# Two batches of triangular inverses on GpSimd, their closing transposes held back, and the latent attention's transfers on SyncE

## The chip, the cores and the metric

One core of a Trainium2 chip runs the whole program. The metric is device time in microseconds (us) for one execution, inputs to output.

The engines are TensorE (PE, with its weight loads as PEld), VectorE (DVE), ScalarE (ACT), GpSimd (POOL) and SyncE (SP). Each takes its instructions in its own program order; a scheduler that runs when the kernel is built fixes that order.

## The reference

Two networks run in series: a two-layer one (`first_block`), and then a diffusion-style one (`second_block`) whose even layer mixes a Gated DeltaNet, run in both directions over the sequence, with a latent attention (MLA). The change touches only that even layer. The part of it that matters, shortened:

```python
def delta_rule_chunked(q, k, v, g, beta, s0):
    ...
    m = jnp.where(strict, jnp.einsum('bhncd,bhnsd->bhncs', kb, kc) * decay, 0.0)
    tmat = lax.linalg.triangular_solve(m + eye, eye, lower=True, unit_diagonal=True)
    u = jnp.einsum('bhncs,bhnsv->bhncv', tmat, vb)
    w = jnp.einsum('bhncs,bhnsk->bhnck', tmat, kb * jnp.exp(gc)[..., None])
    ...
    def step(s, inp):
        v_new = u_i - jnp.einsum('bhck,bhkv->bhcv', w_i, s)
        o_i = jnp.einsum('bhck,bhkv->bhcv', qd_i, s) + jnp.einsum('bhcs,bhsv->bhcv', qk_i, v_new)
        s = s * gl_i[..., None, None] + jnp.einsum('bhck,bhcv->bhkv', kd_i, v_new)

def even_mixer(...):
    o_lat, o_ctx = gdn_bidirectional(...)
    b_lat = blocked_attention(q_l, [k_c, k_l], [v_c, v_l], scale)
    b_ctx = blocked_attention(mla_q(ctx), k_c, v_c, scale)
    y = concatenate([gdn_output(o), b], -1) @ w_out
```

So for each chunk of 64 positions and each of 8 heads the inverse of a unit lower triangular 64x64 matrix is wanted; then a scan goes over the chunks and carries a state.

## The kernel before

Most of the kernel is dense matrix products on PE (`mm3`, L411 to L416). The even layer's stage lies at about 1500 to 1800 us of the span and comes in this order.

**Chunks.** The sequence is 4 blocks of 128 positions (numbers 0 to 3) and the context 2 more (4 and 5). `gdn_chunks` returns seven jobs, which run beside the last input projections (L416). `decays(b)` forms the triangles of block b for both directions and lays their diagonal 32x32 pieces out in a tile of `triW`, four blocks to a batch: batch "ctx" holds blocks 4 and 5 of both directions, batch 0 the blocks 0 to 3 forward, batch 1 the same backward. `triangles` (L1500) transposes a batch on DVE into a work tile A. `invert` (L1502 to L1515) turns A into its inverse X, for all 128 partitions at once: for each of 31 columns a multiply of two broadcast operands into `tm` (L1510) and a subtraction from X (L1511), 62 dependent instructions over tiles of 31 to 256 elements. Then it transposes X back into the batch's `triW` tile (L1513). All of that is on DVE.

A batch's tiles are lent by others. Batch 0 has A = `eo1` and X = `eo2`; batch 1 has A = a spare `triW` tile and X = `eo0`. `eo1` and `eo3` are also where the latent attention later writes its first result for the context.

**Scan.** `gdn_scan` makes four tiles `DT00`, `DT01`, `DT10`, `DT11` (direction, then parity of the walk), zeroed on GpSimd (L1527), and does six walks. Walk i takes one block in each direction. Its `solve` copies the inverted pieces into DT (L1546, ACT, 16 copies), transposes them (L1556, DVE), joins them by two groups of small products (`ng`, L1559 and L1563 on PE) with a copy `ND` (L1560, ACT) between and a copy with sign behind (L1565, ACT), and multiplies them into `sa` (L1575, PE), from which u and w follow. `kd` and `VK` are products on DVE (L1567, L1569). Then four `step`s, two in each direction, carry the states `St` (L1611 to L1633, PE and DVE in turn). Walks 0 and 1 take the context's blocks, so batch "ctx" alone; walk 2 is the first that needs batches 0 and 1.

**Filler.** `mla` is a generator of 12 units of the latent attention, and each walk draws one or two of them (`UNITS`), so that the attention's products lie beside the scan. A unit scores (`S`, L1402, PE), takes maxima and exponentials (L1328, L1332 on DVE; L1335 on ACT), transposes (`ptr`, L1348, PE; copied by ACT and DVE at L1351), weighs (`po`, L1359, PE), scales (`bt`, L1414 and L1415), and stores. Its operands `vp` and `kq` come by transfers that GpSimd issues (L1384, L1388), and its result goes out the same way (L1419) except in the context's units, where `hl` writes it as a high and a low part: a cast on ACT (L398) and a subtraction on DVE (L399), in the first into `eo1` and `eo3`.

The order around the change is the scheduler's. It is a program order for each engine, worked out with estimated durations, and an instruction that waits holds all that stand behind it on its engine.

Of the kernel before, what the change touches and what calls it, by code (L numbers as in the profile page):

```python
# [12 lines left out]
OP = mybir.AluOpType  # L13
# [225 lines left out]
def build(tc, A, out, cst_at, vec_at, chk_at, tap=None, upto=99, mark=lambda n: None):  # L239
    nc = tc.nc  # L240
    V, S, T, G = nc.vector, nc.scalar, nc.tensor, nc.gpsimd
# [11 lines left out]
    def load(dst, src):  # L253
        nc.sync.dma_start(dst, src)
# [358 lines left out]
    x = xp.tile([128, KD, SEQ], F32, name="x", tag="x")  # L613
# [464 lines left out]
    kqD = dram("kqD", [8, 96, 2, TOT])  # L1078
    vD = dram("vD", [4, 128, 6, 128])
    boD = dram("boD", [4, 128, TOT])  # L1080
# [299 lines left out]
    def mla(tp, ctx):  # L1380
        scale = 96.0 ** -0.5
        for p in range(4):
            vp = tp.tile([128, 6, 128], F32, name="vp", bufs=2)
            G.dma_start(vp, vD[p])  # L1384
            KQ = []
            for half in range(2):
                kq = tp.tile([96, 2, TOT], F32, name="kq", bufs=2)
                G.dma_start(kq, kqD[2 * p + half])  # L1388
                KQ.append(kq)
            for qb0, nk, k0, b0 in ((SEQ, CTX, SEQ, 4), (0, TOT, 0, 0), (256, TOT, 0, 0)):  # L1390
                Ps = []
                rsum = tp.tile([128, 4], F32, name="rsum", bufs=3)
                for half in range(2):
                    mx = tp.tile([128, 4], F32, name="mx", bufs=3)
                    row = [tp.tile([128, TOT], F32, name="P", bufs=8)[:, :nk] for _ in range(2)]

                    def score(i):
                        q = KQ[half][:, 1, qb0 + 128 * i:qb0 + 128 * i + 128]
                        for c0 in range(0, nk, 512):
                            c1 = min(c0 + 512, nk)  # L1400
                            pS = bank("S", c1 - c0, "S")
                            T.matmul(pS, q, KQ[half][:, 0, k0 + c0:k0 + c1], start=True, stop=True)  # L1402
                            yield pS

                    soft_rows(row, score, scale, mx, [rsum[:, c:c + 1] for c in (half, 2 + half)])
                    Ps.append(row)
                po = bank("out", 256, "po")
                for _ in weigh(po, Ps, [[(128 * j, 128)] * 2 for j in range(nk // 128)],
                               lambda half, j: vp[:, b0 + j, 64 * half:64 * half + 64], tp, "turn"):
                    pass  # L1410
                V.reciprocal(rsum, rsum)
                rb = on_features(rsum, 2, [256], "turn")[0]
                bt = tp.tile([128, 256], F32, name="bt", bufs=2)
                S.copy(bt, po)  # L1414
                V.tensor_tensor(bt, bt, rb, OP.mult)  # L1415
                if qb0 == SEQ:
                    hl(bt, *(v[:, p] for v in ctx))
                else:
                    G.dma_start(boD[p, :, qb0:qb0 + 256], bt)  # L1419
                yield  # L1420

    batches, batch, inverse, NOc = {}, {}, {}, []

    def off_diagonal(d, a):

# [4 lines left out]
    def gdn_chunks(gp, slots):  # L1430
# [70 lines left out]

        def invert(key, A, X, Y):  # L1502

            parts = batches[key][1]
            V.memset(X, 0.0)
            V.memset(X.rearrange("p y x -> p (y x)")[:, ::33], 1.0)
            for j in range(31):
                n, m = j + 1, 31 - j
                t = gp.tile([128, 256], F32, name="tm", bufs=1)[:, :n * m].rearrange("p (y x) -> p y x", y=m)
                V.tensor_tensor(t, X[:, j:j + 1, :n].to_broadcast([128, m, n]), A[:, n:, j:j + 1].to_broadcast([128, m, n]), OP.mult)  # L1510
                V.tensor_tensor(X[:, n:, :n], X[:, n:, :n], t, OP.subtract)  # L1511
            for d, r in parts:
                V.transpose(Y[r], X[r] if d == 0 else X[r].rearrange("p s c -> p c s"))  # L1513
            inverse[key] = Y

        def inversion(key, A, X):
            triangles(key, A)
# [5 lines left out]

    def gdn_scan(oT, gA, gp, beside, then):
        DTs = [[gp.tile([128, 8, 128], F32, name=f"DT{d}{i}") for i in range(2)] for d in range(2)]
        for t in DTs[0] + DTs[1]:
            G.memset(t, 0.0)  # L1527
        prep = {}

        def solve(i):  # L1530
# [69 lines left out]
        def step(d, b, a, St):  # L1600

            u, wT, kd, eb, qd, qk = prep[d, b]
            rows = halves[a]

            pb = bank("step", 1024, "st").rearrange("p (b c) -> p b c", b=2)
            pw, po, pu = pb[:, :, :256], pb[:, a, 256:], pb[:, 1 - a, 256:]
            for p in range(4):
                for r in halves:  # L1610
                    T.matmul(po[r, 64 * p:64 * p + 64], St[r, p], qd[r, p, rows], start=p == 0, stop=False)  # L1611
            for p in range(4):
                for half, r in enumerate(halves):
                    T.matmul(pw[rows, half, 64 * p:64 * p + 64], wT[r, p, rows], St[r, p], start=half != a, stop=half != a,
                             skip_group_check=half == a)
            vn = gp.tile([128, 8, 64], F32, name="vn", bufs=3)
            by = [v.rearrange("p (i b) t -> p i b t", b=2) for v in (vn[rows], u[rows])]
            V.tensor_tensor(by[0], by[1], pw[rows].rearrange("p b (i t) -> p i b t", i=4), OP.subtract)
            for h in range(8):
                T.matmul(pu[halves[h % 2], 64 * (h // 2):64 * (h // 2) + 64], kd[rows, h], vn[rows, h], start=True, stop=True)  # L1620
            for h in range(8):
                T.matmul(po[halves[h % 2], 64 * (h // 2):64 * (h // 2) + 64], vn[rows, h], qk[rows, 64 * h:64 * h + 64],
                         start=False, stop=h > 5)
            ot = oT[:, :, 128 * b + 64 * a:128 * b + 64 * a + 64]
            o3 = po.rearrange("p (i t) -> p i t", i=4)
            if (b, a) in seen:
                V.tensor_tensor(ot, o3, ot, OP.add)
            else:
                S.copy(ot, o3)
                seen.add((b, a))  # L1630
            last = 64 * a + (63 if d == 0 else 0)
            V.tensor_tensor(St, St, eb[:, :, last:last + 1].to_broadcast([128, 4, 64]), OP.mult)
            V.tensor_tensor(St, pu.rearrange("p (i t) -> p i t", i=4), St, OP.add)  # L1633

        St = []
        for d in range(2):
# [3 lines left out]
        order = [[4, 5, 0, 1, 2, 3], [5, 4, 3, 2, 1, 0]]  # L1640

        def walk(i):
            solve(i)
            for a in range(2):
                for d in range(2):
                    step(d, order[d][i], a if d == 0 else 1 - a, St[d])

        next(beside)
        for i in range(6):
            walk(i)  # L1650
# [525 lines left out]
```

## Time and profile before

| | us |
|---|---|
| median of 3 runs | 3222.15 |
| lowest, highest | 3220.92, 3222.18 |
| the profiled execution's own time | 3223.53 |
| its span | 3221.7 |
| busy PE, DVE, ACT, POOL | 3067.8, 2041.2, 1448.2, 17.4 |

The span is from the first to the last instruction of the profiled execution; 1.83 us of that execution's time lie outside it. Busy times are sums over instructions. Times in the rows below are us from the start of the span, and ns where marked as the mean of one.

### The profile page before, as it was taken

The page shows a single profiled execution, that of the slowest core. Times are in us where ns is not written, and L with a number is a line of the kernel's source. Part 1 is how long each engine was busy: PE and PEld are TensorE (multiplying, and loading weights), DVE is VectorE, ACT ScalarE, POOL GpSimd, SP SyncE. Part 2 cuts the span into 40 slices and gives each one's busy share as a digit, 9 for nine tenths or more (in the row PEclk, how much of TensorE's full clock was granted, in tenths as well). Part 3 has the DMA queues.
Part 4 walks back from the last instruction along what each step waited for, and adds up shares of the span by engine and source line. Part 5 has one row for each costly group of instructions (what it writes and reads, how often), then busy time and mean ns, then how long its engine had stood idle before and what let it go on. Part 6 is the DMA issues. An engine that isn't in the chain of part 4 may idle for free.

```text
span 3221.7 us, 51374 instructions
## 1 busy us (share of the span) xinstructions
PE 3067.8 (95%) x20678; PEld 2605.9 (81%) x20678; DVE 2041.2 (63%) x4021; ACT 1448.2 (45%) x2533; POOL 17.4 (1%) x47
## 2 busy tenths in 40 slices
PE   6999999998999999998899999999997989999998
PEld 5788888975888889876667898888887867898887
DVE  7976555788787777668966674442338347572335
ACT  4965333446553335556554562212124446562223
POOL 0000000000000000000100000000000000000000
PEclk9999999997999999998999999999998999999999
DMA  7556554320266554442322433441223221242232
GB/s 233 190 155 218 194 189 163 125 66 7 74 195 200 188 198 166 131 143 96 107 67 92 142 105 118 165 136 58 67 69 125 79 91 47 76 152 95 95 100 101
DMA packets 137615, 404.11 MB, mean 125 GB/s; under 512 B 13856, under 2 KB 37152, under 8 KB 136736
## 3 DMA queue, kind: packets, MB, share of 16 engines
q1 hardware_dynamic: 135344, 389.81, 36.6%
q0 software_dynamic: 2032, 11.01, 1.1%
q8 instruction: 162, 2.65, 0.3%
q14 instruction: 77, 0.63, 0.1%
HBM read 376.12 MB, written 24.64 MB: 124 GB/s over the span
## 4 chain that ended last, share of the span: by engine, by line
PE 62%; issue 8%; DVE 5%; ACT 4%; DMA 0%; POOL 0%; DVEq 0%; ACTq 0%; POOLq 0%
PE mm L416 49%; PE po L1359 2%; PE rb L547 2%; PE ptr L1348 1%; PE S L830 1%; PE S L1402 1%; PE ss L527 1%; ACT DT L1546 1%; ACT wH L398 1%; PE po L969 1%; PE sa L1575 1%; PE ptr L975 1%; DVE acc L519 1%; DVE wL L399 1%; DVE ct L1683 0%
## 5 line engine op out<-in xcount | busy, mean ns | idle before, releaser
L398 ACT CAST wH<-raw 128x1024 fp32r<-128x1024 f32 (+4 forms) x446 | 451.8, 1015 | 1144.7 <-PE mm L416 786.0
L399 DVE TENSOR_TENSOR wL<-raw,wH 128x1024 fp32r<-128x1024 f32 (+4 forms) x446 | 525.1, 1180 | 377.4 <-ACT wH L398 370.5
L416 PE MATMUL mm<-mH,wH 128*128 128x256 f32 (+1 forms) x1280 | 406.8, 340 | 8.2 <-DVE f L1764 5.8
L416 PE MATMUL mm<-mH,wL 128*128 128x256 f32 (+1 forms) x1280 | 404.1, 339 | 1.9 <-DVE wL L399 1.9
L416 PE MATMUL mm<-mL,wH 128*128 128x256 f32 (+1 forms) x1280 | 404.2, 338 | 0.0
L416 PEld LDWEIGHTS mm<-mH,wH 128*128 128x128 f32 x1280 | 230.7, 190 | 39.5 <-ACT wH L398 6.0
L589 DVE SCALAR_TENSOR_TENSOR raw<-raw,cond_c 128x1024 f32<-128x1024 f32 x128 | 156.6, 1225 | 157.1 <-DMA raw<-in_ada 156.4
L416 PEld LDWEIGHTS mm<-mH,wL 128*128 128x128 f32 x1280 | 229.7, 189 | 30.9 <-DVE wL L399 2.3
L416 PEld LDWEIGHTS mm<-mL,wH 128*128 128x128 f32 x1280 | 230.2, 189 | 28.6
L416 PE MATMUL mm<-f2u0L,wH 128*128 128x512 f32 (+1 forms) x752 | 190.3, 327 | 0.0
L416 PE MATMUL mm<-f2u0H,wH 128*128 128x512 f32 (+1 forms) x752 | 190.0, 326 | 0.0
L416 PE MATMUL mm<-f2u0H,wL 128*128 128x512 f32 (+1 forms) x752 | 189.6, 326 | 0.0
L416 PE MATMUL mm<-f2u1H,wL 128*128 128x512 f32 (+1 forms) x432 | 151.4, 352 | 1.2 <-DVE wL L399 1.1
L416 PE MATMUL mm<-f2u1H,wH 128*128 128x512 f32 (+1 forms) x432 | 150.9, 352 | 0.6 <-ACT nt L1739 0.5
L416 PE MATMUL mm<-f2u1L,wH 128*128 128x512 f32 (+1 forms) x432 | 151.2, 352 | 0.2
L416 PEld LDWEIGHTS mm<-f2u0H,wL 128*128 128x128 f32 x752 | 118.1, 189 | 13.1
L416 PEld LDWEIGHTS mm<-f2u0H,wH 128*128 128x128 f32 x752 | 117.6, 189 | 12.9
L416 PEld LDWEIGHTS mm<-f2u0L,wH 128*128 128x128 f32 x752 | 117.7, 189 | 12.6
L1744 DVE TENSOR_TENSOR nt<-nt,mm 128x512 f32<-128x512 f32 (+1 forms) x52 | 31.5, 605 | 146.8 <-PE mm L416 146.4
L626 DVE SCALAR_TENSOR_TENSOR x<-mm,mod,x 128x256 f32<-128x256 f32 (+1 forms) x112 | 66.1, 597 | 88.5 <-PE mm L416 88.3
L416 PE MATMUL mm<-f0L,wH 128*128 128x512 f32 (+1 forms) x296 | 107.0, 362 | 0.5 <-DVE f0L L565 0.5
L416 PE MATMUL mm<-f0H,wH 128*128 128x512 f32 (+1 forms) x296 | 106.8, 361 | 0.4 <-ACT f0H L564 0.4
(697 smaller groups left out, 7232.9 us busy)
## 6 DMA issues: line engine op xcount, KB each, us to landing
raw<-in_ada SPq DMA_DIRECT2D x192, 512.0 KB, 3.8
raw<-in_fw SPq DMA_DIRECT2D x142, 512.0 KB, 4.1
raw<-in_gw SPq DMA_DIRECT2D x113, 512.0 KB, 3.3
raw<-in_gw SPq DMA_DIRECT2D x34, 384.0 KB, 3.0
raw<-in_owin SPq DMA_DIRECT2D x25, 512.0 KB, 3.2
raw<-in_ewin SPq DMA_DIRECT2D x22, 512.0 KB, 3.3
raw<-in_awin SPq DMA_DIRECT2D x20, 512.0 KB, 3.9
raw<-in_ewout SPq DMA_DIRECT2D x18, 512.0 KB, 3.4
```

Source lines behind the costliest of these rows:

```text
L398: S.copy(H, src)
L399: V.tensor_tensor(L, src, H.bitcast(F32), OP.subtract)
L416: T.matmul(ps, W[w][:, k], h(p, k0 + k, sl), start=first and k == 0 and j == 0, stop=last and k == kt - 1 and j == 2)
L519: V.tensor_tensor(acc[0], acc[0], sq, OP.add)
L527: T.matmul(pc[:, ns * b:ns * b + ns], sq, sel, start=True, stop=True)
L547: T.matmul(pb[r * i:r * i + r, b:b + 128], rs[:, c:c + 1].to_broadcast([128, r]), ident, start=True, stop=True)
L589: V.scalar_tensor_tensor(junk, r, 1.0, c, OP.mult, OP.mult, accum_out=o[:, j:j + 1])
L626: V.scalar_tensor_tensor(x[:, n, sl], ps, gate[:, n:n + 1], x[:, n, sl], OP.mult, OP.add)
L830: T.matmul(ps, q, k[:, sl], start=j == 0, stop=j == 1)
L969: T.matmul(po[64 * half:64 * half + 64], vw[:, kt, :64], PT, start=kt == 0, stop=kt == b)
L975: T.transpose(pt[:, 128 * i:128 * i + 128], Ps[half][i][:, 128 * kt:128 * kt + 128], ident)
L1359: T.matmul(po[64 * half:64 * half + 64], vs[half], PT[:kn, half * w:half * w + w], start=j == 0, stop=j == len(keys) - 1)
```

## The change

1. `invert` works on GpSimd for batches 0 and 1; batch "ctx" stays on DVE. That covers the zeroing of X and the 62 instructions of each.
2. The closing transpose of batches 0 and 1 is put into a function and held in a list, `late`. Both are issued, on DVE, at the start of walk 2, and are ordered behind the last instruction of walk 1's last step.
3. Of the four DT tiles the two of even walks are zeroed on DVE, the two of odd walks on GpSimd as before.
4. `mla`'s loads of `vp` and `kq` and its stores of `bt`, 20 transfers, are issued by SyncE (`load`). In SyncE's order the first unit's `vp` and its two `kq` stand right behind the two loads of walk 1's k, and those wait for DVE's two `VK` products (L1567) of walk 0, whose buffers they take.

```diff
@@ mla @@
-            G.dma_start(vp, vD[p])
+            load(vp, vD[p])
...
-                G.dma_start(kq, kqD[2 * p + half])
+                load(kq, kqD[2 * p + half])
...
-                    G.dma_start(boD[p, :, qb0:qb0 + 256], bt)
+                    load(boD[p, :, qb0:qb0 + 256], bt)
...
-    batches, batch, inverse, NOc = {}, {}, {}, []
+    batches, batch, inverse, NOc, late = {}, {}, {}, [], []
@@ gdn_chunks, invert @@
-            parts = batches[key][1]
-            V.memset(X, 0.0)
-            V.memset(X.rearrange("p y x -> p (y x)")[:, ::33], 1.0)
+
+            E = V if key == "ctx" else G
+            E.memset(X, 0.0)
+            E.memset(X.rearrange("p y x -> p (y x)")[:, ::33], 1.0)
             for j in range(31):
                 n, m = j + 1, 31 - j
                 t = gp.tile([128, 256], F32, name="tm", bufs=1)[:, :n * m].rearrange("p (y x) -> p y x", y=m)
-                V.tensor_tensor(t, X[:, j:j + 1, :n].to_broadcast([128, m, n]), A[:, n:, j:j + 1].to_broadcast([128, m, n]), OP.mult)
-                V.tensor_tensor(X[:, n:, :n], X[:, n:, :n], t, OP.subtract)
-            for d, r in parts:
-                V.transpose(Y[r], X[r] if d == 0 else X[r].rearrange("p s c -> p c s"))
-            inverse[key] = Y
+                E.tensor_tensor(t, X[:, j:j + 1, :n].to_broadcast([128, m, n]), A[:, n:, j:j + 1].to_broadcast([128, m, n]), OP.mult)
+                E.tensor_tensor(X[:, n:, :n], X[:, n:, :n], t, OP.subtract)
+
+            def place():
+                for d, r in batches[key][1]:
+                    V.transpose(Y[r], X[r] if d == 0 else X[r].rearrange("p s c -> p c s"))
+                inverse[key] = Y
+            if key == "ctx":
+                place()
+            else:
+                late.append(place)
@@ gdn_scan @@
-        for t in DTs[0] + DTs[1]:
-            G.memset(t, 0.0)
+        for i in range(2):
+            for d in range(2):
+                (G if i else V).memset(DTs[d][i], 0.0)
...
+            return nc.cur_bb.bb.instructions[-1]
...
         def walk(i):
+            nonlocal done
+            if i == 2:
+                with tc.issue_after(done):
+                    for place in late:
+                        place()
             solve(i)
             for a in range(2):
                 for d in range(2):
-                    step(d, order[d][i], a if d == 0 else 1 - a, St[d])
+                    done = step(d, order[d][i], a if d == 0 else 1 - a, St[d])
```

The line numbers in the order rows below are those of each kernel: the changed kernel's L1511, L1512, L1516, L1535, L1554, L1564, L1568, L1573, L1586 are L1510, L1511, L1513, L1527, L1546, L1556, L1560, L1565, L1578 of the kernel before.

**GpSimd at the start of the scan.** Here are GpSimd's rows before; `vp` and `kq` are the attention's operands, and a number behind a name is a tile's.

```order
L1527 MEMSET DT00_14032 128x1024
L1527 MEMSET DT01_14033 128x1024
L1527 MEMSET DT10_14034 128x1024
L1527 MEMSET DT11_14035 128x1024
L1384 DMA vp_14044<-vD_t_10816 128x768
L1388 DMA kq_14046<-kqD_t_10813 96x1536
L1388 DMA kq_14048<-kqD_t_10813 96x1536
L1384 DMA vp_14975<-vD_t_10816 128x768
```

And here the same engine in the change, in the midst of batch 0's inverse (`eo2` is X, `eo1` is A):

```order
L1511 TENSOR_TENSOR tm_13849<-eo2_12714,eo1_12713 128x220
L1512 TENSOR_TENSOR eo2_12714<-eo2_12714,tm_13849 128x22x10
L1511 TENSOR_TENSOR tm_13852<-eo2_12714,eo1_12713 128x231
L1535 MEMSET DT01_14031 128x1024
L1512 TENSOR_TENSOR eo2_12714<-eo2_12714,tm_13852 128x21x11
L1535 MEMSET DT11_14033 128x1024
L1511 TENSOR_TENSOR tm_13855<-eo2_12714,eo1_12713 128x240
L1512 TENSOR_TENSOR eo2_12714<-eo2_12714,tm_13855 128x20x12
```

The zeroings of `DT01` and `DT11` now stand behind 21 and 22 of batch 0's 62 instructions, and no transfer stands in this queue any more.

**ScalarE at the context's first attention result.** Before, from the copy `bt` to the cast that writes `eo1` (walk 0's copies `eb`, `w_`, `wT` and `oT` stand between):

```order
L1414 COPY bt_14102<-po_14077 128x256
L1335 ACTIVATE P_14439,rsum_14437<-P_14439,mx_14438 128x768
L1591 ACTIVATE eb_14242<-eg_14233 128x512
L1335 ACTIVATE P_14440,rsum_14437<-P_14440,mx_14438 128x768
L1578 COPY w__14250<-sa_14251 128x256
L1578 COPY w__14250<-sa_14258 128x256
L1583 COPY wT_14270<-wt_14265 128x512
L1629 COPY oT_12710<-st_14285 128x4x64
L1335 ACTIVATE P_14458,rsum_14437<-P_14458,mx_14457 128x768
L1591 ACTIVATE eb_14281<-eg_14272 128x512
L1335 ACTIVATE P_14459,rsum_14437<-P_14459,mx_14457 128x768
L1629 COPY oT_12710<-st_14323 128x4x64
L1351 COPY PT_14482<-ptr_14477 128x512
L398 CAST eo1_14023<-bt_14102 128x256
```

In the change:

```order
L1335 ACTIVATE P_14437,rsum_14435<-P_14437,mx_14436 128x768
L1414 COPY bt_14100<-po_14075 128x256
L398 CAST eo1_14021<-bt_14100 128x256
L1599 ACTIVATE eb_14240<-eg_14231 128x512
L1335 ACTIVATE P_14438,rsum_14435<-P_14438,mx_14436 128x768
L1586 COPY w__14248<-sa_14249 128x256
L1586 COPY w__14248<-sa_14256 128x256
```

The cast stands right behind `bt`, 12 rows earlier, ahead of walk 0's `eb` and its second `w_`.

**VectorE and ScalarE at the entry to walk 2.** Before, DVE's closing transpose of batch 1 (X is `eo0`) stood among walk 1's third step and the attention:

```order
L1332 TENSOR_SCALAR mx_15039<-mx_15039 128x1
L1511 TENSOR_TENSOR eo0_12712<-eo0_12712,tm_14009 128x31
L1328 TENSOR_SCALAR P_15059,mx_15058<-S_15061 128x512
L1513 STREAM_TRANSPOSE triW_12711<-eo0_12712 128x1024
L1618 TENSOR_TENSOR vn_14916<-u_14748,st_14899 64x512
L1632 TENSOR_TENSOR St0_14040<-St0_14040,eb_14780 128x256
```

In the change both closing transposes stand behind walk 1's last step, here on DVE from that step's last update of the state `St1`:

```order
L1635 TENSOR_TENSOR oT_12710<-st_14935,oT_12710 128x4x64
L1641 TENSOR_TENSOR St1_14040<-st_14935,St1_14040 128x256
L1351 COPY PT_15120<-ptr_15115 128x512
L1516 STREAM_TRANSPOSE triW_12711<-eo2_12714 128x1024
L1516 STREAM_TRANSPOSE triW_12711<-eo0_12712 128x1024
L1415 TENSOR_TENSOR bt_15136<-bt_15136,rb_15131 128x256
L1564 STREAM_TRANSPOSE Dn_15166<-DT00_14030 32x256 x2
L1564 STREAM_TRANSPOSE Dn_15166<-DT10_14032 32x256
```

and ScalarE's rows behind them, up to the signed copies that release `sa`:

```order
L1554 COPY DT00_14030<-triW_12711 32x8x32 x4
L1554 COPY DT10_14032<-triW_12711 32x8x32 x4
L1554 COPY DT01_14031<-triW_12711 32x8x32 x3
L1335 ACTIVATE P_15493,rsum_15472<-P_15493,mx_15492 128x768
L1554 COPY DT01_14031<-triW_12711 32x8x32
L1568 COPY ND_15167<-ng_15168 128x256
L1335 ACTIVATE P_15494,rsum_15472<-P_15494,mx_15492 128x768
L1554 COPY DT11_14033<-triW_12711 32x8x32
L1335 ACTIVATE P_15584,rsum_15582<-P_15584,mx_15583 128x256
L1573 ACTIVATE DT00_14030<-ng_15168 32x8x32 x2
L1573 ACTIVATE DT10_14032<-ng_15168 32x8x32 x2
```

Both transposes, all copies into DT of walk 2 and its `ND` moved from among walk 1's steps to behind the last of them.

## Rows read from the trace of the kernel before

**Rows 1.** The page's busy times: share of the span and number of instructions of each engine.

```profile
PE 3067.8 (95%) x20678; PEld 2605.9 (81%) x20678; DVE 2041.2 (63%) x4021; ACT 1448.2 (45%) x2533; POOL 17.4 (1%) x47
```

**Rows 2.** Windows (busy us of PE, PEld, DVE, ACT, POOL; PE clock granted; DMA).

```profile
1540.00:1560.00 20.00, 16.11 (x209) 12.26 (x210) 17.95 (x59) 12.00 (x28) 0.00 (x0) 0.79 0.34 96
...
1620.00:1640.00 20.00, 16.16 (x236) 11.03 (x234) 15.95 (x43) 10.80 (x19) 0.00 (x0) 0.91 0.14 41
...
1545.00:1660.00 115.00, 104.78 (x1317) 74.91 (x1317) 95.15 (x306) 62.17 (x135) 4.28 (x8) 0.97 0.26 75
```

**Rows 3.** The chain that ended last, 1545 to 1582 us, by line.

```profile
by line: PE S L1402 19.5%; PE sa L1575 8.8%; PE ptr L1348 8.1%; PE po L1359 7.0%; DVE P L1328 5.6%; ACT DT L1546 5.5%; DVE eo L1511 4.7%; DVE tm L1510 3.7%; issue 3.6%; PE st L1620 3.3%; PE st L1622 3.2%; ACT PT L1351 3.2%; PE st L1611 3.0%
```

**Rows 4.** Groups on DVE, 1520 to 1640 us (busy us, mean ns | idle before).

```profile
L1511 DVE TENSOR_TENSOR eo<-eo,tm 128x31 f32<-128x31 f32 (+15 forms) x62 | 20.8, 336 | 0.5
...
L1510 DVE TENSOR_TENSOR tm<-eo,triW 128x31 f32<-128x31 f32 (+15 forms) x31 | 10.3, 333 | 0.1
...
L1510 DVE TENSOR_TENSOR tm<-eo,eo 128x31 f32<-128x31 f32 (+15 forms) x31 | 10.3, 332 | 0.3
...
L1569 DVE TENSOR_TENSOR kd<-k,kdw 128x512 f32<-128x512 f32 x7 | 4.8, 685 | 0.1
...
L1567 DVE TENSOR_TENSOR VK<-k,egc 128x512 f32<-128x512 f32 x6 | 4.1, 677 | 0.0
```

**Rows 5.** GpSimd: memsets of the line that zeroes DT (ns min/median/max), then its timeline.

```profile
L1527 POOL MEMSET DT<- x4: 951/951/951, 1532.0 to 1534.6; 128x1024 f32 x4
...
73.17 0.10 POOL L750 MEMSET xb<- 128x3 f32 x1 [72.30 <-ACT wH L398]
...
1536.07 1.02 POOL L1388 DMA_DIRECT2D kq<-kqD_t  x2
```

**Rows 6.** DVE's timeline (start, us, what [idle before <-releaser]).

```profile
1526.29 1.23 DVE L1500 STREAM_TRANSPOSE eo<-triW 128x1024 f32<-128x1024 f32 x1
...
1556.94 0.42 DVE L1415 TENSOR_TENSOR bt<-bt,rb 128x256 f32<-128x256 f32 x1
...
1574.43 1.24 DVE L1513 STREAM_TRANSPOSE triW<-eo 128x1024 f32<-128x1024 f32 x1
...
1622.53 1.94 DVE L1513 STREAM_TRANSPOSE triW<-eo 128x1024 f32<-128x1024 f32 x1
```

**Rows 7.** ACT's timeline, walks 0 and 2.

```profile
1532.97 8.97 ACT L1546 COPY DT<-triW 32x256 f32<-32x256 f32 x14
...
1541.97 0.37 ACT L1560 COPY ND<-ng 128x256 f32<-128x256 f32 x1
...
1543.66 1.54 ACT L1565 ACTIVATE DT<-ng 32x256 f32<-32x256 f32 x4
...
1573.52 0.41 ACT L398 CAST eo<-bt 128x256 fp32r<-128x256 f32 x1
...
1624.50 5.13 ACT L1546 COPY DT<-triW 32x256 f32<-32x256 f32 x8 [1.53 <-DVE triW L1513]
...
1629.65 0.94 ACT L1335 ACTIVATE P<-P,mx 128x768 f32<-128x768 f32 x1
```

**Rows 8.** PE's timeline, walk 0 and the entry to walk 2.

```profile
1545.25 2.08 PE L1575 MATMUL sa<-VK,DT 128*128 128x128 f32 x8 [1.68 <-ACT DT L1565]
...
1547.12 1.68 PE L1402 MATMUL S<-kq 96*128 96x256 f32 x4
...
1625.24 0.68 PE L1620 MATMUL st<-vn,kd 64*64 64x64 f32 x16 [0.99 <-DVE vn L1618]
...
1633.65 0.98 PE L1622 MATMUL st<-qk,vn 64*64 64x64 f32 x16
...
1645.08 1.16 PE L1575 MATMUL sa<-VK,DT 128*128 128x128 f32 x8 [0.23 <-ACT DT L1565]
```

**Rows 9.** SyncE's queue, where walk 1's k is loaded.

```profile
1536.05 1.17 SPq L254 DMA_DIRECT2D k<-kM_t  x2
```

**Rows 10.** Transfers issued from 1500 to 1850 us (count, KB each, median us to landing).

```profile
kq<-kqD_t POOLq DMA_DIRECT2D x8, 576.0 KB, 4.8
```

More of the change, by code (lines that the diff above doesn't have):

```diff
@@ L1645, in walk @@
                 for d in range(2):
-                    step(d, order[d][i], a if d == 0 else 1 - a, St[d])
+                    done = step(d, order[d][i], a if d == 0 else 1 - a, St[d])
+        done = None
         next(beside)
```

## The prediction

> **What bounds the kernel now.** I read the page's busy times first: PE is busy for 95% of the span, DVE for 63%, POOL for 1% [rows 1]. So a shorter DVE or an idle POOL is worth something only where PE waits, and the next view is the windows of the stage that the change touches. From 1545 to 1660 us PE works 104.78 of 115 us: 10.2 us of idle time is all that the scan's two first walks could give back, though PE's clock too is below full there, at 0.79 of it from 1540 to 1560 and 0.91 from 1620 to 1640 [rows 2]. Then I read the chain of waits for 1545 to 1582 us, the stretch of batch 0's inverse. It runs through PE for most of its length, but the inverse's own lines, eo L1511 and tm L1510, hold 4.7% and 3.7% of it [rows 3]: now and then PE waits for something that stands behind them in DVE's queue. The groups on DVE say how much of such work there is: 62 multiplies of 332 and 333 ns, 62 subtractions of 336 ns, so 41.4 us for the two batches [rows 4].
>
> **The inverse on GpSimd.** No row shows a POOL instruction with two inputs, so its duration p is bounded. Not below DVE's: 0.333 us and some 0.03 for the handover between dependent instructions, 0.37 [rows 4]. Above: a POOL memset of 1024 elements takes 0.951 us, and the inverse's instructions have 176 elements on average (the sum of n times m over 31 columns is 5456) [rows 5]. I take 0.57, nearest to the memset rows: 3 elements in the first column cost 0.10, 1024 cost 0.951, so 0.83 ns an element; two inputs and one output at that pace make 176 x 3 x 0.83 = 0.44, and 0.10 to start and 0.03 to hand over come on top [rows 5].
> The Trainium skill (GPSIMD Engine Reference, section 3.1, Elementwise: side-by-side cycle accounting) has measured this very operation at 1.96 times VectorE's time, for 2048 elements. By that p would be an estimated 0.65, and the sum below 5 us higher, 3238; no row here shows it.
> Batch 0 starts once DVE has transposed its triangles, at 1526.29 + 1.23 = 1527.5 [rows 6]. Two memsets of DT stand among its instructions, 1.9 us [rows 5]. The 61st of its 62 instructions, the last that reads eo1, thus ends at 1527.5 + 61 x 0.57 + 1.9 = 1564.2 (1552 at p = 0.37, 1587 at 0.95). Batch 1 follows with 62 x 0.57 = 35 us and is done at about 1600, before walk 2 wants it at 1635: no cost.
>
> **Its two costs.** *The start.* DT01's zeroing stands behind 21 of POOL's instructions (142 elements each on average): 1527.5 + 21 x (0.13 + 142 x 3 x 0.83 ns) = 1537.7, and 0.95 for itself, 1538.6. ACT has eight copies into DT00 and DT10 first, at 8.97 / 14 = 0.64 each from 1532.97, until 1538.1 [rows 7]. So ACT waits 0.5, and a third copy into DT11, 0.64, now stands ahead of ND: ND and the first sa come 1.1 us later than 1541.97 and 1545.25 [rows 7, 8]. *The cast.* In the old order it ran at 1573.52, when DVE had just finished batch 0 [rows 7]. In the new one it stands right behind bt, so it is reached when the multiply of bt ends, at 1556.94 + 0.42 = 1557.4, plus the 1.1 [rows 6]. It must wait for POOL's last read of eo1, until 1564.2: 5.7 us, and its own 0.41 then lies on the path. Behind it on ACT stand eb and the second w_ of walk 0; on DVE the subtraction into eo3 waits for the cast and holds the maxima of the next scores. PE can do two more score products and stops. So start and cast together cost 1.1 + 5.7 + 0.4 = 7.2 us. The ends: 1.5 if p is at most 0.475, where 61 instructions are done by 1558.4; 30 at p = 0.95.
>
> **What DVE gains.** 41.4 us of work leave DVE. On the path lay 4.7% and 3.7% of 37 us, 3.1 [rows 3], and PE's wait of 0.99 for vn at 1625.24, which stood behind batch 1's closing transpose of 1.94 [rows 6, 8]. I take -4.1. The far end is all of PE's idle time in 1545 to 1660, -10.2 [rows 2]; the near end is 0, since a wait of PE for DVE may only turn into one for ACT.
>
> **The late transposes.** Before, batch 0's stood at 1574.43 and batch 1's at 1622.53, and the copies into DT ran from 1624.50, under walk 1's third and fourth step [rows 6, 7]. Walk 1's last products ended at 1633.65 + 0.98 = 1634.6 and walk 2's sa began at 1645.08, 10.5 us later, with PE busy in between [rows 8]. Now everything follows the last step in a row. From its end: a copy of 0.7 on DVE, the first transpose 1.24, thirteen copies into DT at 0.64 (8.3), three exponentials of about 1 us with their sums (3.0), ND 0.37, four signed copies 1.54 [rows 6, 7]; with 0.7 for handovers that makes 15.8 us to sa. Recurrence alone: +5.4. PE has only about 6 us of products placed in that gap, against 10 before, so it idles 15.8 - 6 - 0.5 = 9.3 more. The attention's products that it did earlier instead come back as filler somewhere, but not surely: I take the middle, +7.4. The ends are 0, if the filler covers the entry, and 11.7: 9.3, plus a lower clock after the gap as at 1540 to 1560, (0.21 - 0.09) x 20 = 2.4 [rows 2].
>
> **The transfers.** POOL loses some 10 us of issuing, but was idle. SP issues the first unit's three loads behind walk 1's two loads of k, which went out at 1536.05 for 1.17 us, waiting for VK [rows 9]. Three more at 0.58 or less end by 1539.0, and a kq lands 4.8 later, 1543.8 [rows 10]; the first score product runs at 1547.12 [rows 8]. That gap of 3.3 us covers it: 0. If POOL had kept them, they would stand behind the inverse. Later units have longer still. Zeroing DT00 and DT10 on DVE, at the scan's start where DVE has lost its inverse: 0.
>
> **Sum.** +7.2 - 4.1 + 7.4 = +10.5 on the profiled execution's 3223.53, so 3234.0; that execution stood 1.4 above the median of the runs, 3222.15. Forecast: **3233** us. With p from 0.475 to 0.75 and the entry between its ends this case covers 3221 to 3244.
>
> **Rivals.**
> *Shared access to SBUF* (slower still). If POOL and DVE can't both read SBUF, DVE's products of two SBUF operands shut POOL out and the other way round. For it: there are 13 such products in two groups, kd and VK, at 0.68 us each [rows 4]. Against it: no row shows both engines at work. Seven of them fall beside batch 0, 7 x 0.68 = 4.8 on the cast's wait; and 13 times DVE waits for half an instruction of POOL, 13 x 0.29 = 3.7: 3241.
> The Trainium skill (SBUF: State Buffer, section Who interferes with whom) states such a lock for a DVE instruction with two SBUF inputs against a GpSimd instruction that reads SBUF.
> *A quick GpSimd and a covered entry* (faster). If p is 0.47 or less, the cast finds eo1 free; 0.475 is the point that decides. If then the filler covers the entry to walk 2, PE's whole idle time of 10.2 us can go: 1.5 - 10.2 = -8.7, so 3213. For it: DVE is busy for 95 of the 115 us of the two walks [rows 2] and loses 41. Against it: p would have to be within 0.1 of DVE's own, and the new order puts nothing long beside the entry.
> *A quick GpSimd and an uncovered entry.* 1.5 - 4.1 + 7.4 = +4.8: 3227.
> *The order is not what binds.* If the transposes' place is hidden as the old one was, while the cast waits, the sum is 3.1: 3225; it belongs to the first case's lower end.
>
> **How the numbers follow.** Less than 0.2%, 6.4 us, can't be told from no change here: below 3215.7 is faster, above 3228.6 slower. The summed case gets 0.5 (slower 0.38, same 0.11, faster 0.01), shared access 0.2 (slower), the quick and covered one 0.15 (faster 0.12, same 0.03), the quick and uncovered one 0.15 (same 0.10, slower 0.05). That makes faster 0.13, same 0.24, slower 0.63. The range 3215 to 3248 leaves out about 0.1 of the quick case below, and above it a slow p or both costs at their far ends.
>
> **What would show it.** POOL's row for the inverse: mean 0.57, and 0.475 the point below which I am wrong. ACT idle for some 6 us ahead of the cast, released by POOL, and PE idle with it near 1560. Sixteen us from walk 1's last product to walk 2's sa, PE idle for more than half. No wait of PE for kq. If walk 2's sa comes within 11 us of walk 1's end, the late transposes cost nothing and the middle I took is wrong; if DVE's kd and VK grow from 0.68, the shared access is there.

## The result and the profile after

The changed kernel takes 3247.88 us (median of 4 runs, 3246.39 to 3249.01) against 3221.96 before: 1.0074 times the time, 95% interval 1.0062 to 1.0086. It is slower by 25.9 us; the forecast was 3233, with a range to 3248 whose upper end the result just meets. The profiled execution took 3247.34 us, span 3245.5.

Two waits of ScalarE from 1530 to 1700 us are ended by GpSimd: the copies' wait for the zeroing of DT01, and the cast's wait for the inverse. Both are waits that the change made: the kernel before has none there. On ACT's timeline (start, us, what [idle before <-releaser]):

```profile
1536.85 5.12 ACT L1554 COPY DT<-triW 32x256 f32<-32x256 f32 x8 [0.75 <-DVE DT L1535]
1544.66 4.45 ACT L1554 COPY DT<-triW 32x256 f32<-32x256 f32 x7 [2.69 <-POOL DT L1535]
...
1565.30 0.37 ACT L1414 COPY bt<-po 128x256 f32<-128x256 f32 x1 [0.32 <-PE po L1359]
1571.36 0.41 ACT L398 CAST eo<-bt 128x256 fp32r<-128x256 f32 x1 [5.68 <-POOL tm L1511]
```

The cast, at 1573.52 in [rows 7], is now right behind ACT's copy to bt, and ACT stands 5.68 us ahead of it. The first 0.55 of these it needed anyway, for DVE's product into bt, which ended at 1566.23:

```profile
1565.81 0.42 DVE L1415 TENSOR_TENSOR bt<-bt,rb 128x256 f32<-128x256 f32 x1 [0.83 <-PE rb L547]
```

So the inverse alone made it wait 5.1. GpSimd's groups, 1500 to 1700 us, answer [rows 4]:

```profile
L1512 POOL TENSOR_TENSOR eo<-eo,tm 128x31 f32<-128x31 f32 (+15 forms) x62 | 35.2, 568 | 4.8
L1511 POOL TENSOR_TENSOR tm<-eo,eo 128x31 f32<-128x31 f32 (+15 forms) x31 | 17.1, 553 | 17.8 <-DVE eo L1500 15.5
```

An instruction is busy for 0.55 to 0.57 us. Two places on GpSimd's timeline with the same 135 elements:

```profile
1534.13 1.06 POOL L1511 TENSOR_TENSOR tm<-eo,eo 128x135 f32<-128x135 f32 x1
...
1567.53 0.42 POOL L1511 TENSOR_TENSOR tm<-eo,eo 128x135 f32<-128x135 f32 x1
```

The longer one ran beside two products of DVE, which took 0.79 each, not the 0.685 of [rows 4]:

```profile
1534.16 1.58 DVE L1577 TENSOR_TENSOR kd<-k,kdw 128x512 f32<-128x512 f32 x2
```

Walk 0's first and second sa and the entry to walk 2 on PE, beside [rows 8]:

```profile
1552.29 2.07 PE L1583 MATMUL sa<-VK,DT 128*128 128x128 f32 x8 [1.65 <-ACT DT L1573]
...
1572.31 2.02 PE L1583 MATMUL sa<-VK,DT 128*128 128x128 f32 x8 [4.26 <-ACT eb L1599]
...
1643.94 0.63 PE L1630 MATMUL st<-qk,vn 64*64 64x64 f32 x16
...
1660.32 2.08 PE L1583 MATMUL sa<-VK,DT 128*128 128x128 f32 x8 [0.76 <-ACT DT L1573]
```

From walk 1's end at 1644.57 to sa: 15.75 us, 10.45 before. Where the whole stage's time went is told by two windows that I laid over it in each kernel, from the last input product (L416) to the first output product (first number the length, then PE busy). Before, and after:

```profile
1532.04:1800.35 268.31, 244.71 (x3504) 179.30 (x3505) 193.57 (x567) 140.19 (x294) 13.71 (x23) 0.96 0.29 90
```

```profile
1535.30:1820.11 284.81, 255.34 (x3506) 188.45 (x3505) 168.56 (x447) 141.71 (x294) 67.26 (x117) 0.91 0.29 88
```

The stage is 16.5 us longer with the same instructions on PE. Of that PE is idle for 5.9 more (29.5 against 23.6), and **busy for 10.6 more**: the granted clock is 0.91, not 0.96. It fell in these windows of the changed kernel:

```profile
1540.00:1560.00 20.00, 9.07 (x148) 7.56 (x148) 7.24 (x18) 10.63 (x20) 18.27 (x27) 0.53 0.46 126
...
1640.00:1660.00 20.00, 16.52 (x255) 10.43 (x253) 13.99 (x37) 15.76 (x31) 0.00 (x0) 0.86 0.28 82
1660.00:1680.00 20.00, 18.08 (x166) 13.88 (x168) 9.61 (x24) 13.91 (x29) 0.00 (x0) 0.89 0.25 80
1680.00:1700.00 20.00, 20.00 (x366) 16.18 (x363) 7.19 (x16) 6.31 (x16) 0.00 (x0) 0.71 0.13 43
```

The granted clock has two levels, 2.4 GHz (full) and 1.2 (half): at 0.53 nearly all of the window ran at half. PE had had nothing for 3.6 us from the last input product on, and within the window it stood for 6.0 us until ND came. From 1640 to 1700 us the shares missing make (0.14 + 0.11 + 0.29) x 20 = 10.8 us of full speed; the kernel before lost 1.8 there. The steps of the scan lie elsewhere in each kernel, so a window from walk 1's end compares them better. Its first 20 us, before and after:

```profile
1634.63:1654.63 20.00, 18.11 (x194) 12.41 (x195) 13.02 (x40) 13.81 (x30) 1.59 (x3) 0.94 0.38 107
```

```profile
1644.57:1664.57 20.00, 16.19 (x195) 10.92 (x194) 12.67 (x35) 18.17 (x37) 0.00 (x0) 0.74 0.17 51
```

Of the span's 23.8 us, 7.3 lie outside the stage: 3.3 ahead of it and 4.0 behind. Over all profiles here the stage's start lies between 1532.0 and 1542.8 us, and where PE's order is the same up to 1420 us its clock already differs; I put those 7.3 to no part of the change.

### The profile page after: what moved, and what is told of

Read it like the earlier page. It is cut to its first block, busy times and chain, and to the rows that moved or that the text cites. A ratio compares the mean times of both kernels' runs of the same rounds, so it can differ in the third digit from the quotient of the medians.

```text
span 3245.5 us, 51371 instructions
## 1 busy us (share of the span) xinstructions
PE 3084.1 (95%) x20678; PEld 2621.3 (81%) x20678; DVE 2013.2 (62%) x3895; ACT 1448.7 (45%) x2533; POOL 76.4 (2%) x153
## 4 chain that ended last, share of the span: by engine, by line
PE 68%; DVE 6%; ACT 4%; issue 1%; POOL 1%; DMA 0%; DVEq 0%; ACTq 0%; SPq 0%
PE mm L416 53%; PE rb L547 2%; PE po L1359 2%; PE ptr L1348 2%; PE S L830 1%; PE ss L527 1%; PE S L1402 1%; ACT wH L398 1%; PE sa L1583 1%; PE po L969 1%; PE ptr L975 1%; DVE wL L399 1%; DVE c L1227 1%; POOL tm L1511 1%; POOL eo L1512 1%
## 5 line engine op out<-in xcount | busy, mean ns | idle before, releaser
L416 PE MATMUL mm<-mH,wH 128*128 128x256 f32 (+1 forms) x1280 | 407.2, 340 | 8.6 <-DVE f L1779 5.8
L416 PE MATMUL mm<-mH,wL 128*128 128x256 f32 (+1 forms) x1280 | 404.6, 339 | 1.5 <-DVE wL L399 1.5
L416 PE MATMUL mm<-mL,wH 128*128 128x256 f32 (+1 forms) x1280 | 404.6, 339 | 0.0
L416 PEld LDWEIGHTS mm<-mH,wH 128*128 128x128 f32 x1280 | 230.9, 190 | 39.9 <-ACT wH L398 6.2
L416 PEld LDWEIGHTS mm<-mH,wL 128*128 128x128 f32 x1280 | 230.1, 190 | 30.5 <-DVE wL L399 1.9
L416 PEld LDWEIGHTS mm<-mL,wH 128*128 128x128 f32 x1280 | 230.6, 190 | 28.5
L416 PE MATMUL mm<-f2u0L,wH 128*128 128x512 f32 (+1 forms) x752 | 190.4, 327 | 0.0
L416 PE MATMUL mm<-f2u0H,wH 128*128 128x512 f32 (+1 forms) x752 | 190.1, 326 | 0.0
L416 PE MATMUL mm<-f2u0H,wL 128*128 128x512 f32 (+1 forms) x752 | 189.6, 326 | 0.0
L416 PE MATMUL mm<-f2u1H,wL 128*128 128x512 f32 (+1 forms) x432 | 151.5, 353 | 1.2 <-DVE wL L399 1.1
L416 PE MATMUL mm<-f2u1H,wH 128*128 128x512 f32 (+1 forms) x432 | 151.0, 352 | 0.6 <-ACT nt L1754 0.5
L416 PE MATMUL mm<-f2u1L,wH 128*128 128x512 f32 (+1 forms) x432 | 151.2, 352 | 0.1
L416 PEld LDWEIGHTS mm<-f2u0H,wL 128*128 128x128 f32 x752 | 118.0, 189 | 13.2
L416 PEld LDWEIGHTS mm<-f2u0H,wH 128*128 128x128 f32 x752 | 117.8, 189 | 12.8
L416 PEld LDWEIGHTS mm<-f2u0L,wH 128*128 128x128 f32 x752 | 117.8, 189 | 12.6
L416 PE MATMUL mm<-f0L,wH 128*128 128x512 f32 (+1 forms) x296 | 107.1, 362 | 0.5 <-DVE f0L L565 0.5
L416 PE MATMUL mm<-f0H,wH 128*128 128x512 f32 (+1 forms) x296 | 106.8, 361 | 0.4 <-ACT f0H L564 0.4
```

Of the source, the lines that this page charges most:

```text
L416: T.matmul(ps, W[w][:, k], h(p, k0 + k, sl), start=first and k == 0 and j == 0, stop=last and k == kt - 1 and j == 2)
```

## The experiments

The base is the changed kernel, unless said. Each ratio is to the kernel before, with its 95% interval. "Stage" is the same window: length, PE idle in it, PE busy in it, all from one profiled execution. The two executions of the changed kernel differ there by 0.1 us of idle time but 3.0 of busy time, so a difference in busy time of about 3 us between two rows is not clear of noise. The profiled executions of e3 and e6 took 7.4 and 6.5 us more than their medians.

| run | ratio | stage | idle | busy |
|---|---|---|---|---|
| before | 1 | 268.3 | 23.6 | 244.7 |
| change, first profile | 1.0074 (1.0062 to 1.0086) | 284.8 | 29.5 | 255.3 |
| e5 change again | 1.0065 (1.005 to 1.008) | 281.9 | 29.6 | 252.3 |
| e1 inverse on DVE | 1.0016 (1.0007 to 1.0026) | 270.6 | 22.6 | 248.0 |
| e2 cast held | 1.0021 (1.0011 to 1.0031) | 271.2 | 25.1 | 246.0 |
| e3 transposes earlier | 1.0009 (0.9997 to 1.002) | 272.4 | 27.1 | 245.3 |
| e4 DT on DVE | 1.0032 (1.0021 to 1.0044) | 277.2 | 28.2 | 249.0 |
| e6 no waits | 0.998 (0.9969 to 0.999) | 265.4 | 18.1 | 247.3 |
| e7 SyncE only | 1.0005 (0.9995 to 1.0015) | 269.7 | 23.2 | 246.5 |
| e8 transposes at once | 1.0129 (1.0114 to 1.0144) | 307.3 | 56.0 | 251.3 |
| e9 wide products | 1.0057 (1.004 to 1.0074) | 284.6 | 29.9 | 254.7 |
| e10 one batch | 1.0058 (1.0039 to 1.0078) | 286.2 | 39.3 | 246.9 |
| e11 one batch, own tm | 1.0012 (1.0003 to 1.0022) | 269.6 | 23.9 | 245.6 |
| e12 as e11, DT split | 1.0006 (0.9996 to 1.0015) | 269.5 | 27.6 | 241.9 |

**e1: the inverse back on DVE.**

```diff
-            E = V if key == "ctx" else G
+            E = V
```

> Both inverses back on DVE; the late closing transposes, the transfers on SyncE and the split zeroing of DT stay. My theory (three waits: DT01's zeroing behind the inverse, the cast behind the inverse, the late entry to walk 2) leaves only the third here: walk 1's end to walk 2's first sa about 15.8 us as in the changed kernel, against 10.5 before, and 3228 to 3236 us. Rival, shared access to SBUF as the main loss: back within 3 us of the kernel before, 3222 to 3225. Rival, SyncE's queue as the main loss: still 3240 or more, with PE waiting for kq or vp.

3231.28 us, within my range and above the rival of shared access. The late entry is there (walk 1's end at 1636.21, sa at 1654.37: 18.2 us), yet the stage is only 2.3 us longer: 3.3 more of busy time, and idle time 1.0 less. PE fills that gap with the attention's products. By the stage the late transposes, with the transfers and the split zeroing that stay in this run, cost less than the 7.4 that I took; by the whole time it is 5.2 us (1.0016), and the interval, 2 to 8, does not exclude 7.4.

**e2: the cast held.** The context's first `hl` is called behind walk 0, ordered behind its last state update on DVE and its last copy on ACT.

```diff
-                    hl(bt, *(v[:, p] for v in ctx))
+                    put = lambda bt=bt, p=p: hl(bt, *(v[:, p] for v in ctx))
+                    held.append(put) if p == 0 else put()
...
+            if i == 0:
+                with tc.issue_after(done), tc.issue_after(copied[-1]):
+                    held[0]()
```

> As the change, but the cast and the subtraction of the context's first attention result stand behind walk 0's last step. My theory: the 5.7 us wait of the cast for GpSimd goes, walk 0's second sa comes some 6 us earlier, 3240 to 3244 us. Rival, shared access: GpSimd's inverse stays as long and DVE and GpSimd still shut each other out, 3246 to 3249.

3232.8 us, better than I expected: against the change (e5) the stage lost 10.7 us, 4.5 of them idle time, 6.3 clock. Walk 0's second sa came 4.6 us earlier than in e5, counted from the last input product, not some 6. The cast's wait is a cause; its price was more than the wait.

**e3: the transposes earlier.**

```diff
-            if i == 2:
-                with tc.issue_after(done):
-                    for place in late:
-                        place()
...
+                    if (i, a, d) in ((0, 1, 1), (1, 0, 1)):
+                        with tc.issue_after(done):
+                            late[i]()
```

> As the change, but batch 0's closing transpose stands behind walk 0's last step and batch 1's behind walk 1's second. My theory: walk 1's end to walk 2's sa falls from 15.8 to 10 to 12 us, and the later walks lose less, 3236 to 3243 us. Rival, the order does not bind there (PE has other work in that gap): 3246 to 3249.

3228.71 us, below my range too. The entry fell to 6.8 us (walk 1's end 1655.38, sa 1662.16). Again the clock (7.0 us of busy time against e5) gave back more than idle time (2.5). The cast still waited 5.7 us.

**e4: all of DT zeroed on DVE.**

```diff
-                (G if i else V).memset(DTs[d][i], 0.0)
+                V.memset(DTs[d][i], 0.0)
```

> As the change, but all four DT tiles are zeroed on DVE. My theory: ACT no longer waits 2.7 us for GpSimd's zeroing of DT01, PE's clock falls less after the gap, ND and the first sa come 3 to 4 us earlier; the cast then waits as much longer, since batch 0 ends only 1.9 us earlier: 3244 to 3247 us. Rival, the start is a loss of its own that nothing behind it hides: 3243 or less.

3237.23 us, a miss, on the rival's side of 3243. By the waits, though, my account held; ACT's waits for GpSimd in this run are

```profile
ACT eo L398 <- POOL tm L1511: 9.8, 1, 9.8
```

alone: DT01's wait is gone and the cast's is 4.1 longer. Counted from the last input product, the first sa comes only 1.8 us earlier than in e5, not 3 to 4, the second 1.2 later, and walk 2's first 0.3 later. So up to there nothing was won, against the rival. The stage's 4.7 us against e5, 1.4 of idle time and 3.3 of busy time, come behind that point, where the edit itself does nothing; why is open.

**e5: the change again**, beside e6 to e8.

> The changed kernel once more, as the base of its parts. If the three waits add up as I first put it, 3246 to 3250 us again (1.0065 to 1.0085 of the kernel before), and the last three experiments show that each wait removed also gives back a low PE clock. Rival, that the low clock of 0.71 from 1680 to 1700 us in the first profile is an accident of that execution's timing: 3236 to 3243 us, and the stage from the last input projection to the output projection is 8 to 12 us longer than before, not 16.5.

3245.69 us, just under my range: the loss is the change's, and so is the low clock, 0.87, 0.88 and 0.83 in the three windows from 1640 us. The third was 0.71 in the first profile, so some 2.4 us of the loss there belonged to that execution alone.

**e6: all three waits out**, the edits of e2, e3 and e4 together.

> As the change, with all three waits out: the cast behind walk 0's last step, batch 0's closing transpose there too, batch 1's behind walk 1's second step, all DT tiles zeroed on DVE. My theory: what is left is DVE's relief, the stage is 2 to 6 us shorter than before: 0.998 to 1.0 of the kernel before. Rival, shared access: GpSimd and DVE still hold each other up, and the cast and transposes are late anyway, 1.001 to 1.004.

3218.04 us, **faster than the kernel before**, by 0.2%. No wait of ACT or DVE for GpSimd is left from 1530 to 1700 us; the stage is 2.9 us shorter, with 5.5 less idle time and 2.6 more busy time (within the noise). I put the gain down to the 41.4 us that leave DVE, but that is not shown: e6 also moves the cast and the transposes, and no run moved them alone in the kernel before.

**e7: only the transfers moved**, on the kernel before.

```diff
-            G.dma_start(vp, vD[p])
+            load(vp, vD[p])
...
```

The loads of `kq` and the stores of `bt` are changed the same way.

> The kernel before with its 20 attention transfers on SyncE and nothing else. My theory: no difference, within 0.1% of the kernel before. Rival, SyncE's queue delays kq or the loads of the walks: 2 to 6 us slower, with PE waiting for a transfer.

3224.54 us, no difference. No wait of PE for a transfer appears.

**e8: the transposes at once.**

```diff
-            if key == "ctx":
-                place()
-            else:
-                late.append(place)
+            place()
```

> As the change, but the closing transposes are issued at once, as in the kernel before, and the scheduler places them: on DVE both now stand ahead of walk 0's first step. My theory: DVE stands still until GpSimd is done with batch 0 (1571 us) and again with batch 1 (1611 us), 3250 to 3275 us. Rival, the late transposes are the main loss and the scheduler does better alone: 3228 to 3240.

3265.67 us, as expected. DVE's waits, 1500 to 1700 us:

```profile
DVE triW L1516 <- POOL eo L1512: 32.2, 2, 19.1
```

The scheduler puts both transposes where DVE must stand and wait, as if GpSimd were faster than it is; what durations it reckons with no run shows. The change's `late` list prevents that: within this change the late place is a gain.

**e9: wide products beside the entry.**

```diff
+            if i == 2:
+                for _ in range(8):
+                    T.matmul(pg, ident, qk[0][:, :256], start=True, stop=True)
             S.copy(ND, pn.rearrange("p (h c) -> p h c", h=8))
```

> As the change, with 8 wide products without use (128x256, into the half of a PSUM tile that is overwritten next) on PE between walk 2's two groups of small products, beside its wait for ND. My theory: the stage lost 8 to 11 us in PE's granted clock and 6 in idle time, and the clock falls because of what the late entry leaves PE to do; these products hold it up: granted clock from 1640 to 1700 us at 0.95 or more, against 0.87, 0.88 and 0.83, and 3 to 6 us less than the changed kernel, 3239 to 3243 us. Rival, they only add work: the clock as it was, and 1 to 3 us more, 3246 to 3250.

3245.61 us, between the two, a miss: 0.95 was not reached. The first 20 us from walk 1's end in e9:

```profile
1646.68:1666.68 20.00, 15.85 (x202) 11.07 (x202) 11.41 (x26) 16.38 (x30) 0.00 (x0) 0.92 0.19 51
```

There the clock was 0.92, against 0.74 in the change; while the products ran it stayed full. Later it fell again: from 1680 to 1720 us e9 lost 5.2 us of full speed, e5 3.4 and the first profile 6.8. And the products themselves took 3.7 us of PE, so nothing was won. What PE is given in the gap does move the clock; what that gives back was less than I took.

**e10: one batch on GpSimd**, with the edits of e4 and e8.

```diff
-            E = V if key == "ctx" else G
+            E = G if key == 1 else V
```

> Only batch 1 on GpSimd, batch 0 back on DVE; closing transposes issued at once and placed by the scheduler (batch 1's behind walk 0's last step), all DT tiles zeroed on DVE, transfers on SyncE. My theory: GpSimd's batch is done by 1572 us, ahead of anything that wants it, the cast waits for DVE as in the kernel before, DVE is relieved of 20.7 us: the stage 1 to 4 us shorter than before, 0.998 to 1.0 of the kernel before. Rival, shared access: DVE's inverse (two operands in SBUF) beside GpSimd's stretches both, batch 0 is late for the cast, 1.001 to 1.004.

3244.5 us, a miss that neither theory foresaw. GpSimd's waits, 1500 to 1700 us:

```profile
POOL tm L1511 <- DVE eo L1512: 66.3, 1, 66.3
```

`tm` has one buffer, held by DVE's batch 0, so the batches ran in turn and batch 1 ended at about 1617, with DVE standing at its transpose for 19.3 us.

**e11: one batch with a buffer of its own.** As e10, but batch 1's products go into its own triW tile, free until the closing transpose, which stands behind walk 0's last step. The edit of the buffer:

```diff
-                t = gp.tile([128, 256], F32, name="tm", bufs=1)[:, :n * m].rearrange("p (y x) -> p y x", y=m)
+                t = Y.rearrange("p y x -> p (y x)") if key == 1 else gp.tile([128, 256], F32, name="tm", bufs=1)
+                t = t[:, :n * m].rearrange("p (y x) -> p y x", y=m)
```

> e10 mended: in e10 GpSimd's batch waited 66 us for the one buffer of tm that DVE's batch held. Here batch 1 puts its products into its own triW tile, and its closing transpose stands behind walk 0's last step. My theory: GpSimd is done with it by 1575 us and nothing waits for it; PE's start is still some 3 us late, since DVE zeroes DT beside batch 0; the stage within 3 us of before, 0.998 to 1.002. Rival, shared access: DVE's and GpSimd's inverses run side by side with two operands in SBUF each, both lengthen by half or more, batch 0 ends after the cast wants it, 1.002 to 1.006.

3230.14 us, inside my range, with the rival's mechanism in full view. GpSimd's groups, and then DVE's from 1530 to 1600 us:

```profile
L1513 POOL TENSOR_TENSOR eo<-eo,triW 128x31 f32<-128x31 f32 (+15 forms) x31 | 20.6, 664 | 2.4
L1512 POOL TENSOR_TENSOR triW<-eo,triW 128x31 f32<-128x31 f32 (+15 forms) x31 | 19.8, 640 | 21.6 <-issue 19.3
```

```profile
L1513 DVE TENSOR_TENSOR eo<-eo,tm 128x31 f32<-128x31 f32 (+15 forms) x31 | 13.3, 428 | 0.3
L1512 DVE TENSOR_TENSOR tm<-eo,eo 128x31 f32<-128x31 f32 (+15 forms) x31 | 13.0, 419 | 0.1
```

Side by side DVE's instructions grow from 336 and 332 ns to 428 and 419, by 26 to 27%, GpSimd's from 568 and 553 (the change) to 664 and 640, by 16 to 17%. Over the stage DVE's busy time fell only from 193.6 us to 189.3, though 20.7 us of instructions left it (3.6 of zeroing came). As built here, half the work on GpSimd is worth less than all of it in e6, which also holds the cast back.

**e12: as e11, with DT01 and DT11 zeroed on GpSimd**, as in the change.

> As e11, but DT01 and DT11 zeroed on GpSimd in the midst of batch 1's inverse, as in the change. My theory: ACT waits 2 to 3 us for DT01 as in the changed kernel, no cast wait follows that would hide it, DVE has 1.8 us less: within 2 us of e11. Rival, the start wait costs its whole 2.7 us: 3 us more than e11.

3226.92 us. The stage is e11's within 0.1 us, and the runs' intervals overlap. But the wait that I expected is not there: ACT waits 0.7 us for DT01, not 2 to 3, so this run does not tell what the start's wait costs. PE is idle 3.7 us more than in e11 and busy 3.7 less, with the same granted clock over the stage (0.96); why is open.

## Why the prediction was right, and where its sizes were off

**The pace of GpSimd.** I took p = 0.57. The busy time came out at that (0.553 and 0.568), but the handover was 0.07 to 0.08 us, not 0.03: an instruction of 0.49 at 1565.26 is followed at 1565.83. From 1530.88 to 1571.65, less two memsets of 0.95, batch 0's 62 instructions took 0.63 each. Its 61st ended 40.5 us after the batch's start, not 36.7. Against DVE's 0.334, busy time is 1.67 times as long. The Trainium skill's ratio of 1.96 (GPSIMD Engine Reference, section 3.1, for 2048 elements) lies above that of these small tiles, but the estimate of p that I drew from it, 0.65, was nearer to the pace than my 0.57.

**The start.** Priced at 1.1 us; sa came 3.8 later, counted from the last input product (13.2 to 17.0). Two things were mis-sized: ACT's first copies waited for DVE's zeroing of DT00, which I had costed at nothing (1.55 us from the last product to the first copy, 0.93 before), and DT01 waited 2.69, not 0.5, since the first 21 instructions took 12.8 us, not 10.2. Some of them ran beside DVE's kd and VK. The wait for DT01 is hidden behind the cast's: without it (e4) the cast waits 4.1 longer and walk 0's second sa is no earlier.

**The cast.** Forecast wait 5.7, from the end of DVE's product into bt; measured from there 5.1. That it came so near is partly luck: both sides were late by almost the same, the inverse by 3.9 us and bt by 4.5, counted from the last input product. Start and cast together made walk 0's second sa 9.7 us late, not 7.2.

**DVE's gain.** Forecast -4.1. From walk 0's second sa to walk 1's end the lag shrinks from 9.7 us (27.3 and 37.0 from the last input product) to 6.7 (102.6 and 109.3): -3.0. In e6 idle time is 5.5 us less than before, in part perhaps by its other edits.

**The late entry.** 15.8 us forecast, 15.75 measured. The price put on it was wrong: PE idled not 9.3 us more but 3.6 (3.80 of 15.75, 0.23 of 10.45), since the scheduler kept more of the attention for that gap, and some of it ran at half clock (0.81 over the gap, 0.88 before). As delay the entry cost 15.75 - 10.45 = 5.3. Alone it made the stage 2.3 us longer (e1).

**The clock** is the term that the sum mis-sized. I let it into the upper end only, at 2.4 us. It made 10.6 of the stage's 16.5 us (7.6 of 13.6 in e5). That also tells in what form the single edits gave back more than their waits: e2, e3 and e4 regain 4.5, 2.5 and 1.4 us of idle time, but 6.3, 7.0 and 3.3 of busy time. One part of it goes with the late entry: in the first 20 us from walk 1's end the clock was 0.74 in all five profiles that keep the late transposes without added products (the change, e5, e1, e2, e4), so 5.2 us of full speed lost, but 0.94 before, 0.91 in e7 and 1.00 in e3, e6, e10, e11 and e12. Idle time alone does not explain it: PE idles 1.9 us of these 20 both before and in e1. e9 shows that wide products in the gap raise the clock there. Why it falls again later in the change, in e5 and in e9 is open.

**The transfers** at 0: e7 agrees. **Shared access**, a rival at 0.2, is real, and part of the case that came: single rows of the change (1.06 against 0.42) and e11's groups show it. The Trainium skill (SBUF: State Buffer, section Who interferes with whom) says that a DVE instruction with two SBUF inputs contends with a GpSimd instruction that reads SBUF; these rows agree. In batch 0 six instructions beside DVE's kd and VK took 2.3 us more, taken together, than those of the same size elsewhere in it, the larger part of the 3.9 by which the inverse was late. But that alone does not make the loss: e6 keeps both batches on GpSimd and is faster than before. **The quick GpSimd**, 0.15, fell with p; its end, without the cast's wait and with the entry covered, is what e6 built by hand: 3218.04, where I had put it at 3213.

So the sum of 10.5 was right in its signs, and as delays along the scan its terms were near: +9.7 at walk 0's second sa (7.2 forecast), -3.0 up to walk 1's end (-4.1) and +5.3 at the entry (7.4) make 12.0 at walk 2's sa (12.2 in e5). From there to the stage's end another 4.5 came (1.4 in e5), in which PE's idle time is no longer than before and the clock 0.93, not 0.99. That part, and the 7.3 us outside the stage, no term described. Cut the other way, the same 16.5 are 5.9 of idle time and 10.6 of clock.

That the time fell inside the range is luck as well. The forecast rise was 10.9 us, the measured one 25.9. My summed case was to end at 3244, with p at 0.75; only with the entry at its far end, which I had not put into that figure, does it reach 3248. And the room above was meant for a slow p or for both costs at their far ends, not for what came: a low clock and 7.3 us elsewhere.

## What to carry to other kernels

When work moves to a slower engine, look for every buffer and wait that ended when the old engine was done: here the scheduler put the waiting instructions early on other engines (the cast on ACT, in e8 both transposes on DVE), and each held all behind it. Order the readers behind a step that is surely later, as e6 does; with the zeroing moved too, that turned a loss of 0.65 to 0.74% into a gain of 0.2%. Price a wait of PE not by its idle time alone, but with the granted clock behind it.

## What was not expected of the hardware

GpSimd's product of two operands took 0.24 us at 31 elements and 0.64 at 256, about 1.8 ns an element, plus 0.07 to 0.08 between dependent instructions. Two engines with two SBUF operands each slow each other in both directions (26 to 27% and 16 to 17%, e11). In the stage of the changed kernel PE's clock took more than PE's waits did (10.6 and 5.9 us). And with the same 1.9 us of idle time in 20, PE's granted clock was 0.94 before and 0.74 in e1: it fell there with no more idle time to show for it.
